# A hybrid attention and matrix-memory layer on one core: the output weights split in the first half and kept in two parts, matrix memory rows transposed at the chunk's end, the gate as tanh, another order of the projections

## The chip, the cores and the metric

The kernel runs on one core of a Trainium2 chip. The metric is the device time of one execution in microseconds (us); the kernel before took 1369.46 us in the median of three runs (1366.92 to 1369.54). A core has TensorE (PE, with its weight loads as PEld), VectorE (DVE), ScalarE (ACT), GpSimd (POOL) and SyncE (SP), which here issues all transfers. The engines run at the same time, each through its own instructions in a fixed order.

## The reference

One layer over 2048 rows of width 1024. All groups read one projection of x, each group's output is gated, and the three outputs are joined, projected and normalised:

```python
u = x @ w_in
(fq, fk, fv, ff, fz, mq, mk, mv, mi, mf, mo, mz, rq, rz) = jnp.split(u, split_points, axis=-1)
y_fox = forgetting_attention(fq, fk, fv, ff + fox_f_bias) * jax.nn.silu(fz)
...
y_ml = mlstm(mq_c, mk_c, mv, mi + i_bias, mf + f_bias, mo, norm_g) * jax.nn.silu(mz)
...
y_mem = memory_attention(rq, mem_k, mem_v) * jax.nn.silu(rz)
y = jnp.concatenate([y_fox, y_ml, y_mem], axis=-1) @ w_out
return layer_norm(DEEPNORM_ALPHA * x + y, ln_g, ln_b)
```

The first group is causal attention (6 heads of 64) with a cumulative forget bias. The second is a matrix memory (4 heads of 96) that goes through the rows in chunks and carries a state; in it h = sigmoid(o) * h, then each head is normalised (variance + 1e-5) and multiplied by norm_g. The third attends to 256 memory tokens (4 heads of 64).

## The kernel before, in words

**Precision.** Most products are made of three: an operand is rounded to a high part and the rest is kept as a low part, and high x high, low x high and high x low are summed in PSUM. So a weight tile that arrives by DMA in `raw` is split: ACT writes the high part `h`, DVE writes the low part `l` (`load_part`, line 454). The output weights of rows 384 to 767 also take the gain `norm_g` in this step (`ng_sb`).

**Stages.** The rows are two halves of 1024 (`hf`), each of two blocks of 512 (`bi`). The list `SEQ` (line 302) names the projection jobs in order for each half: `gate` (forget and input gates, attention's values), `mk`/`mv` (memory keys and values), `rq` (memory queries), `y` and `z` (gates), `h0` to `h5` (one attention head's queries and keys), `r` (matrix memory values and gates, by rows) and `c` (its queries and keys, by columns, with a convolution of four taps). A suffix `.0` or `.1` is one block alone. `u0.0` to `u3.0` in the second half lend weight buffers to the first four matrix-memory chunks.

**Attention** of a block of 512 queries of one head is an item: `att_max` computes all scores once for the maxima (PSUM `mx`, 2 banks, DVE reduces each into `mp`), `att_qk` computes them again shifted (PSUM `st`), ACT takes the exponentials twice (`ph`, `p`), DVE subtracts to the low part `pl`, POOL sums `p` into `acc` for the denominator, and `att_pv` multiplies by the values (PSUM `o`). Items follow each other in a fixed order. Keys of the first half are written to DRAM and read again for the second (`km_scr`, `kb_scr`); the block's own keys are copied by DMA (`km<-kb`, and two rows `km<-c_scr`).

**Matrix memory.** A chunk of 128 rows is one `ml_unit` (line 912), 16 in all. It reads its queries, keys, rows and gates from DRAM, makes five products in PSUM `pj` (3 banks, shared with all projections), updates the state, normalises, multiplies by the gate and writes `y_scr`.

**Output.** When the projections have freed the x buffers, `out_loads` (line 1266) loads the 16 tiles of the output weights (8 row groups by 2 column halves of 512), splitting each. `out_tile` (line 1306) handles 128 rows: it loads the transposed attention outputs from `yt_scr` in two parts (5 of the 8 row groups), loads the matrix memory's rows from `y_scr`, transposes them on PE into `st`, splits them (ACT `yh`, DVE `ylo`), multiplies by the output weights, adds alpha * x and normalises.

**What sets the order.** Every step is a generator; `Machine` (line 135) plays them against a table of costs and writes each engine's instructions in the order that this gives. Among ready steps the smallest priority (`PRIO`, line 296) goes first. On the chip that order is fixed. Every instruction is recorded by line 220 (`op.fn(...)`), so the profile is read by tile names. SP issues DMAs strictly in that order, and each waits for its data and for its buffer.

Of the kernel before, what the change touches and what calls it, by code (L numbers as in the profile page):

```python
# [12 lines left out]
F32 = mybir.dt.float32  # L13
# [3 lines left out]
ALU = mybir.AluOpType  # L17
# [259 lines left out]
class Engine:  # L277
# [5 lines left out]
    def __getattr__(self, fn):  # L283
# [11 lines left out]

PRIO = dict(load=0, wo=1.5, post=1, fin=2.5, pv=3, qk=4, mx=1.5, proj=7.5, ml=7, out=9, ln=-0.5)

# [3 lines left out]

SEQ = ("gate0 mk0.0 mk1.0 mv2.0 y0 r0 rq0 rq1.0 rq1.1 h0 y1 z0.0 h1 z0.1 z1 h2 h3 r1 h4 h5 r2 c0 c2 c5 z2 c1 c4.0 c3 c4.1",
       "rq1 rq0.1 y1 rq0.0 gate0 h0 y0.0 y0.1 r2 h1 z0 h2 r1 h3 r0 c0 u1.0 z1 u0.0 c1 h4 c4 c2 u2.0 c5.0 z2 c3 h5 c5.1 u3.0")

# [19 lines left out]
def kernel(ctx: ExitStack, tc: tile.TileContext, xt, x, wg, memt, wm, wo, cw, gb, ng, lg, lb, out):  # L324
# [96 lines left out]
    d_scr = [dram([LH, 4], F32, f"d_scr{b}") for b in range(NBLK)]  # L421
    y_scr = [dram([BLK, LW], F32, f"y_scr{b}") for b in range(NBLK)]
    yt_scr = [[dram([P, 5, BLK], F32, f"yt_scr{b}_{i}") for i in range(2)] for b in range(NBLK)]
    km_scr, kb_scr, v_scr = {}, {}, {}
# [4 lines left out]
    def loader():  # L429
        k = 0  # L430
        while True:
            yield lambda: k < len(loads)
            if loads[k] is None:
                late.append("x")
                return
            if len(loads[k]) == 2:

                tt, tag = loads[k]
                k += 1
                lent = yield [Alloc("w", [P, BLK], F32, "u") for _ in range(UNIT)]  # L440
                m.slots[tag] = [(m.wr[t.tensor.name][0], i, t) for i, t in enumerate(lent)]
                heapq.heapify(m.slots[tag])
                spawn(ml_unit(tt, 0, LH, tag), PRIO["ml"])
                continue
            src, ncol, tag, box, key, gain = loads[k]
            if k == wo_box["first"]:
                done.add("w")
            k += 1
            raw, hi, lo = yield [Alloc(RAW0 if k <= START else RAW, [P, BLK], F32, "raw"), Alloc(tag, [P, BLK], F32R, "h"),
                                 Alloc(tag, [P, BLK], F32R, "l")]  # L450
            spawn(load_part(src, ncol, raw, hi, lo, box, key, gain),
                  PRIO["load" if k <= wo_box["first"] else "wo"])

    def load_part(src, ncol, raw, hi, lo, box, key, gain):
# [435 lines left out]
    def ml_rows(g, tt, t_):  # L890
# [21 lines left out]
    def ml_unit(tt, h0, nh, tags):  # L912
# [73 lines left out]
        yield DVE.tensor_scalar(rs, mv[:, :, 1], EPS, 4.0, op0=ALU.add, op1=ALU.mult)  # L986
        yield POOL.tensor_tensor(rs2, rs, mhalf[:, 0:nh], op=ALU.pow)
# [148 lines left out]
    def rq_job(hf, w, xa, g, bi):  # L1136
# [4 lines left out]
        def post(t_):  # L1141
# [3 lines left out]
            for hh in range(2):  # L1145
# [120 lines left out]
    def out_loads():  # L1266
        wo_box.update(box={}, first=len(loads))
        for g in range(2):
            for k in KORDER:

                gain = ng_sb[:, k - 3:k - 2] if 3 <= k < 6 else None
                loads.append((wo[:, k * D + g * BLK:k * D + (g + 1) * BLK], BLK,
                              ["x"] + late if len(loads) - wo_box["first"] < EARLY else "x", wo_box["box"],
                              (KORDER.index(k), g), gain))
        loads.append(None)

# [29 lines left out]
    def out_tile(tt):  # L1306
# [3 lines left out]
        yl = yield [Alloc(["v"] + late, [P, 512], F32R, "ylo") for _ in range(2)]  # L1310
        for i, y_ in enumerate((yh, yl)):
            yield dma(out=y_[0].rearrange("p (k t) -> p k t", k=4), in_=yt_scr[b][i][:, 0:4, cs])
            yield dma(out=y_[1][:, LW:512], in_=yt_scr[b][i][:, 4, cs])
        yr = yield Alloc(late, [P, BLK], F32, "yr")
        yield dma(out=yr[:, 0:LW], in_=y_scr[b][cs, :])
        t_ = yield Alloc("st")
        yield [PE.transpose(t_[:, k * P:(k + 1) * P], yr[:, k * P:(k + 1) * P], ident) for k in range(3)]
        free(yr)
        yield ACT.copy(yh[1][:, 0:LW], t_[:, 0:LW])
        yield DVE.tensor_tensor(yl[1][:, 0:LW], t_[:, 0:LW], yh[1][:, 0:LW].bitcast(F32), op=ALU.subtract)  # L1320
        free(t_)
        zz = yield [Alloc(["raw"] + late, [P, BLK], F32, "xr") for _ in range(2)]
# [119 lines left out]
```

## Time and profile before

| | us |
|---|---|
| median of 3 runs (lowest, highest) | 1369.46 (1366.92, 1369.54) |
| the profiled execution | 1363.92 |
| its span in the trace | 1362.2 |
| PE busy | 1311.0 |
| DVE busy | 1029.7 |
| ACT busy | 650.1 |
| POOL busy | 487.8 |

The first half's projections fill about the first 480 us. The last projection job ends at 1053 us, the last attention item about 1183 us. Output tiles start at 1084.6 us, run among the attention items and have PE for themselves at the end. A matmul in the profile counts as busy until its modelled end, so neighbours overlap; lost time in PE is better read from the share of busy time in a short window together with the clock that was granted.

### The profile page before, as it was taken

How to read it: one execution, taken by the hardware profiler on the slowest of the kernel's cores; microseconds unless marked ns; L12 is line 12 of the kernel's file. 1: busy time of each engine (PE TensorE's matmuls, PEld its weight loads, DVE VectorE, ACT ScalarE, POOL GpSimd, SP SyncE). 2: the span in 40 equal slices, each digit the busy share in tenths (PEclk: the TensorE clock that was granted, in tenths of full speed). 3: DMA queues.
4: the chain of work that ended last, by engine and by line, in shares of the span. 5: the costliest groups of instructions: out<-in, count | busy, mean ns of one | idle time of the engine just before them, and what ended most of it. 6: DMA issues, size and time to landing. Idle time of an engine off the chain costs nothing.

```text
span 1362.2 us, 20386 instructions
## 1 busy us (share of the span) xinstructions
PE 1311.0 (96%) x6648; PEld 1110.4 (82%) x6648; DVE 1029.7 (76%) x2082; ACT 650.1 (48%) x1371; POOL 487.8 (36%) x430
## 2 busy tenths in 40 slices
PE   8999999999999999999999999999999798999997
PEld 7998878888888878979887889877877686788886
DVE  6647888776866688579687878988988877667755
ACT  6325545353454455323635546564565456565400
POOL 3000245242330102112526556353254178564400
PEclk9999999999999999999999999999999598999999
DMA  7614332405222452451320421315414734779642
GB/s 257 215 58 123 99 96 75 132 30 184 76 86 85 152 171 91 150 153 52 105 59 19 155 67 43 99 52 149 148 31 134 217 93 139 215 232 246 196 159 77
DMA packets 136666, 167.54 MB, mean 123 GB/s; under 512 B 13760, under 2 KB 90832, under 8 KB 136560
## 3 DMA queue, kind: packets, MB, share of 16 engines
q1 hardware_dynamic: 136560, 166.24, 39.6%
q8 instruction: 53, 0.87, 0.3%
q14 instruction: 53, 0.43, 0.1%
HBM read 107.05 MB, written 50.29 MB: 116 GB/s over the span
## 4 chain that ended last, share of the span: by engine, by line
PE 77%; DVE 12%; DMA 4%; issue 3%; ACT 2%; POOL 1%; SPq 1%; DVEq 0%; ACTq 0%; POOLq 0%
PE pj L220 57%; PE st L220 8%; PE o L220 7%; PE mx L220 5%; DVE cv L220 2%; DVE pl L220 2%; DVE l L220 2%; DMA dd<-m_scr 1%; DVE mp L220 1%; DMA raw<-in_wg_dram 1%; DMA raw<-in_xt_dram 1%; SPq L220 1%; DVE r L220 1%; POOL acc L220 1%; DVE mx L220 1%
## 5 line engine op out<-in xcount | busy, mean ns | idle before, releaser
L220 POOL TENSOR_TENSOR acc<-acc,p 128x512 f32<-128x512 f32 (+2 forms) x232 | 318.7, 1374 | 426.3 <-ACT p L220 204.9
L220 PE MATMUL pj<-h,h 128*128 128x512 f32 (+3 forms) x1144 | 424.1, 371 | 7.3 <-ACT h L220 6.5
L220 PE MATMUL pj<-h,l 128*128 128x512 f32 (+3 forms) x1144 | 418.8, 366 | 0.8 <-DVE l L220 0.7
L220 PE MATMUL pj<-l,h 128*128 128x512 f32 (+3 forms) x1144 | 419.1, 366 | 0.1
L220 PEld LDWEIGHTS pj<-h,h 128*128 128x128 f32 x1144 | 216.7, 189 | 33.3 <-ACT h L220 6.7
L220 PEld LDWEIGHTS pj<-l,h 128*128 128x128 f32 x1144 | 216.3, 189 | 28.2 <-DVE l L220 1.0
L220 PEld LDWEIGHTS pj<-h,l 128*128 128x128 f32 x1144 | 215.8, 189 | 27.2 <-DVE l L220 2.0
L220 DVE TENSOR_TENSOR pl<-p,ph 128x512 fp32r<-128x512 f32 (+2 forms) x184 | 175.3, 956 | 37.9 <-ACT p L220 33.8
L220 ACT ACTIVATE ph<-st 128x512 fp32r<-128x512 f32 (+2 forms) x219 | 120.3, 556 | 99.6 <-PE st L220 80.5
L220 DVE TENSOR_TENSOR l<-raw,h 128x512 fp32r<-128x512 f32 (+2 forms) x194 | 127.0, 681 | 31.4 <-ACT h L220 30.3
L220 ACT CAST h<-raw 128x512 fp32r<-128x512 f32 (+2 forms) x194 | 108.9, 586 | 70.9 <-DMA raw<-in_wg_dram 48.7
L220 ACT ACTIVATE p<-st 128x512 f32<-128x512 f32 (+2 forms) x232 | 125.9, 545 | 32.7 <-POOL acc L220 18.1
L220 PE MATMUL mx<-km,qm 66*128 66x512 f32 (+2 forms) x304 | 104.3, 380 | 11.1 <-DVE mp L220 9.5
L220 PE MATMUL o<-pl,v 128*128 128x512 f32 (+2 forms) x272 | 103.5, 384 | 7.8 <-DVE pl L220 7.1
L220 PE MATMUL st<-qb,kb 128*128 128x512 f32 (+2 forms) x272 | 109.4, 402 | 0.0
L220 DVE TENSOR_REDUCE mp<-mx 128x1 f32<-128x512 f32 x144 | 95.9, 684 | 16.7 <-PE mx L220 14.6
L220 PE MATMUL st<-qm,km 68*128 68x512 f32 (+2 forms) x272 | 103.2, 379 | 4.6 <-ACT p L220 4.6
L220 PE MATMUL pj<-h,yh 128*128 128x512 f32 (+1 forms) x264 | 106.7, 404 | 0.0
L220 PE MATMUL pj<-h,ylo 128*128 128x512 f32 (+1 forms) x264 | 103.0, 390 | 0.0
L220 PE MATMUL pj<-l,yh 128*128 128x512 f32 (+1 forms) x264 | 102.9, 390 | 0.0
L220 POOL TENSOR_TENSOR y<-y,zs 128x512 f32<-128x512 f32 x20 | 28.8, 1441 | 172.7 <-DVE zs L220 86.2
L220 PE MATMUL o<-ph,v 128*128 128x512 f32 (+2 forms) x219 | 82.4, 380 | 0.9 <-ACT ph L220 0.9
(199 smaller groups left out, 1937.9 us busy)
## 6 DMA issues: line engine op xcount, KB each, us to landing
raw<-in_wg_dram SPq DMA_DIRECT2D x76, 256.0 KB
raw<-in_wg_dram SPq DMA_DIRECT2D x48, 192.0 KB
v<-v_all SPq DMA_DIRECT2D x36, 256.0 KB
raw<-in_xt_dram SPq DMA_DIRECT2D x32, 256.0 KB
xr<-in_x_dram SPq DMA_DIRECT2D x32, 256.0 KB
out_dram<-xr SPq DMA_DIRECT2D x32, 256.0 KB
v_all<-vs SPq DMA_DIRECT2D x16, 384.0 KB
row_scr<-stg SPq DMA_DIRECT2D x32, 192.0 KB
```

The costliest lines, as they stand in the source:

```text
L220: op.fn(*op.args, **op.kw)
```

## The change

1. **Output weights.** Four steps `o0` to `o3` stand in the first half's list; each loads and splits four of the 16 tiles in buffers of the tag `w` and writes both parts to DRAM (`out_split`, `kept`). At the end `load_again` loads two finished parts for each tile, without ACT or DVE.
2. **Matrix memory rows.** The chunk itself transposes its 128 x 384 result on PE (into `pj`), splits it (ACT `yh`, DVE `yl`) and writes both parts to `yt_scr`, which now has all 8 row groups; the memory attention's two groups lie in places 3 and 7. `out_tile` loads two parts in four DMAs and has no transpose, no split and no `y_scr`.
3. **Gate as tanh.** The gate's `0.5 * tanh + 0.5` (one DVE instruction per 128 rows) is gone; the chunk multiplies by (1 + tanh), twice the sigmoid, and its 1e-5 becomes 4e-5 accordingly.
4. **Priority.** The first four chunks have priority 3 in place of 7.
5. **Order.** Both lists of `SEQ` are new.

```diff
-PRIO = dict(..., mx=1.5, proj=7.5, ml=7, out=9, ln=-0.5)
+PRIO = dict(..., mx=1.5, proj=7.5, ml=7, unit=3, out=9, ln=-0.5)
...
-       "rq1 rq0.1 y1 rq0.0 gate0 h0 y0.0 y0.1 r2 h1 z0 h2 r1 h3 r0 c0 u1.0 z1 u0.0 c1 h4 c4 c2 u2.0 c5.0 z2 c3 h5 c5.1 u3.0")
+       "rq1 rq0 y1 gate0 h0 z0 y0 r2 h1 h2 r1 h3 r0 c0 u1.0 z1 u0.0 c1 h4 c5.0 c4 c2 c3 u2.0 z2 c5.1 h5 u3.0")
...
+        if kept is not None:
+            for i, t_ in enumerate((hi, lo)):
+                yield dma(out=kept[i][:, :], in_=t_[:, 0:ncol])
+                if box is None:
+                    free(t_)
+            kept.append("stored")
+
+    def load_again(ncol, hi, lo, box, key, kept):
+        yield lambda: len(kept) == 3
+        for i, t_ in enumerate((hi, lo)):
+            yield dma(out=t_[:, 0:ncol], in_=kept[i][:, :])
+        box[key] = (hi, lo)
...
-            if g == 1:
-                yield DVE.tensor_scalar(o_, o_, 0.5, 0.5, op0=ALU.mult, op1=ALU.add)
-            else:
+            if g == 2:
...
-        yield DVE.tensor_tensor(hg, nd[:, :, 0:LD], hg, op=ALU.mult)
+        yield DVE.scalar_tensor_tensor(hg, hg, 1.0, nd[:, :, 0:LD], op0=ALU.add, op1=ALU.mult)
...
-        yield dma(out=y_scr[b][s * P:(s + 1) * P, h0 * LD:(h0 + nh) * LD], in_=gz[:, 0:nh * LD])
-        free(so, gz)
+        t_ = yield Alloc("pj")
+        yield [PE.transpose(t_[:, k * P:(k + 1) * P], gz[:, k * P:(k + 1) * P], ident) for k in range(3)]
+        free(gz)
+        parts = yield [Alloc(small, [P, ws], F32, s_) for s_ in ("yh", "yl")]
...
+        yield ACT.copy(h_, t_[:, 0:LW])
+        yield DVE.tensor_tensor(l_, t_[:, 0:LW], h_.bitcast(F32), op=ALU.subtract)
...
+    def out_split(n):
+        for g, i in WO_ORDER[4 * n:4 * n + 4]:
+            k = KORDER[i]
+            gain = ng_sb[:, k - 3:k - 2] if 3 <= k < 6 else None
+            wo_parts[g, i] = stored(f"wo{k}_{g}", BLK)
+            loads.append((wo[...], BLK, "w", None, None, gain, wo_parts[g, i]))
```

The order moves at two places that the prediction speaks of. The first is DVE just after the last projection, where the maxima of the last two attention items are reduced (`mp<-mx`). Before, the splits of the output weights (`l<-raw`) stand among them, and a chunk's state update (`cst`):

```order
L220 TENSOR_REDUCE mp_2779_11724<-mx_2782_11728 128x1
L220 SCALAR_TENSOR_TENSOR l_2764_11677<-raw_2762_11675,ng_sb_95,h_2763_11676 128x512
L220 CAST rr_2789_11750<-mx_2787_11745 8x128
L220 SCALAR_TENSOR_TENSOR cst0_182<-cst0_182,dec0_1087,pj_2777_11718 96x97 x2
L220 SCALAR_TENSOR_TENSOR cst1_183<-cst1_183,dec0_1087,pj_2777_11718 96x97 x2
L220 SCALAR_TENSOR_TENSOR l_2770_11695<-raw_2768_11693,ng_sb_95,h_2769_11694 128x512
L220 TENSOR_REDUCE mp_2779_11724<-mx_2788_11748 128x1
L220 SCALAR_TENSOR_TENSOR l_2776_11712<-raw_2774_11710,ng_sb_95,h_2775_11711 128x512
L220 TENSOR_TENSOR l_2786_11739<-raw_2784_11737,h_2785_11738 128x512
L220 TENSOR_REDUCE mp_2779_11724<-mx_2790_11755 128x1
```

Now, at the same item's reduces, DVE has no split of weights; between the reduces stand steps of two chunks (`dd`, and `u`, the lent buffers of the fourth):

```order
L220 TENSOR_REDUCE mp_2816_11873<-mx_2821_11883 128x1
L220 SCALAR_TENSOR_TENSOR sc_2780_11771<-sc_2780_11771 128x4
L220 CAST rr_2824_11897<-mx_2822_11889 8x128
L220 TENSOR_REDUCE mp_2816_11873<-mx_2823_11891 128x1
L220 TENSOR_REDUCE mp_2816_11873<-mx_2825_11901 128x1
L220 TENSOR_REDUCE mp_2816_11873<-mx_2826_11905 128x1
L220 TENSOR_TENSOR dd_2795_11816<-pj_2828_11917,dd_2795_11816 128x512
L220 TENSOR_REDUCE mp_2816_11873<-mx_2827_11911 128x1
L220 TENSOR_REDUCE mp_2816_11873<-mx_2831_11927 128x1
L220 TENSOR_TENSOR u_2664_11360<-u_2663_11359,u_2664_11360 128x384
```

So the splits moved out, into the first half, and the chunks' steps moved up. The second place is SP at the end of the projections. Before, the own keys of the last head's first block (`km0<-kb`, `km0<-c_scr`) stand ahead of, or among, the first loads of output weights (`raw<-in_wo_dram`):

```order
L220 DMA km0_102<-kb_2676_11422 64x512
L220 DMA raw_2688_11451<-in_wo_dram 128x512
L220 DMA raw_2691_11454<-in_wo_dram 128x512
L220 DMA raw_2694_11457<-in_wo_dram 128x512
L220 DMA y_scr0_170<-u_2478_10567 128x384
L220 DMA u_2681_11444<-qk_scr0_134 96x4x128
L220 DMA km0_102<-c_scr2_160 2x512
```

Now the own keys (here `km1`) stand behind the last ten loads of kept parts (`wo6_1` to `wo7_1`, `_h` high and `_l` low):

```order
L220 DMA u_2664_11360<-row_scr3_141 128x384
L220 DMA h_2752_11677<-wo6_1_h_196 128x512
L220 DMA l_2753_11678<-wo6_1_l_197 128x512
L220 DMA h_2754_11679<-wo3_1_h_206 128x512
L220 DMA l_2755_11680<-wo3_1_l_207 128x512
L220 DMA h_2756_11681<-wo4_1_h_208 128x512
L220 DMA l_2757_11682<-wo4_1_l_209 128x512
L220 DMA h_2758_11683<-wo5_1_h_210 128x512
L220 DMA l_2759_11684<-wo5_1_l_211 128x512
L220 DMA h_2760_11685<-wo7_1_h_212 128x512
L220 DMA l_2761_11686<-wo7_1_l_213 128x512
L220 DMA km1_103<-kb_2773_11734 64x512
```

What moved is the key copy: it is now queued behind ten loads of 256 KB. All in all SP has 64 DMAs more: 32 stores and 32 loads of the kept parts, 16 more stores of chunks and 16 fewer loads of output tiles; the 16 loads of the raw output weights stand in the first half.

More of the change, by code (lines that the diff above doesn't have):

```diff
@@ L294 @@
 YTAGS = ("ta", "pl", "ph")
-PRIO = dict(load=0, wo=1.5, post=1, fin=2.5, pv=3, qk=4, mx=1.5, proj=7.5, ml=7, out=9, ln=-0.5)
+PRIO = dict(load=0, wo=1.5, post=1, fin=2.5, pv=3, qk=4, mx=1.5, proj=7.5, ml=7, unit=3, out=9, ln=-0.5)
 EARLY = 3
@@ L421 @@
     d_scr = [dram([LH, 4], F32, f"d_scr{b}") for b in range(NBLK)]
-    y_scr = [dram([BLK, LW], F32, f"y_scr{b}") for b in range(NBLK)]
-    yt_scr = [[dram([P, 5, BLK], F32, f"yt_scr{b}_{i}") for i in range(2)] for b in range(NBLK)]
+    yt_scr = [[dram([P, KT, BLK], F32, f"yt_scr{b}_{i}") for i in range(2)] for b in range(NBLK)]
     km_scr, kb_scr, v_scr = {}, {}, {}
@@ L442, in loader @@
                 heapq.heapify(m.slots[tag])
-                spawn(ml_unit(tt, 0, LH, tag), PRIO["ml"])
+                spawn(ml_unit(tt, 0, LH, tag), PRIO["unit"])
                 continue
-            src, ncol, tag, box, key, gain = loads[k]
+            src, ncol, tag, box, key, gain, *kept = loads[k]
             if k == wo_box["first"]:
@@ L448, in loader, with load_part @@
             k += 1
+            if src is None:
+                hi, lo = yield [Alloc(tag, [P, BLK], F32R, s_) for s_ in "hl"]
+                spawn(load_again(ncol, hi, lo, box, key, *kept), PRIO["load" if k <= wo_box["first"] else "wo"])
+                continue
             raw, hi, lo = yield [Alloc(RAW0 if k <= START else RAW, [P, BLK], F32, "raw"), Alloc(tag, [P, BLK], F32R, "h"),
                                  Alloc(tag, [P, BLK], F32R, "l")]
-            spawn(load_part(src, ncol, raw, hi, lo, box, key, gain),
+            spawn(load_part(src, ncol, raw, hi, lo, box, key, gain, *kept),
                   PRIO["load" if k <= wo_box["first"] else "wo"])
-    def load_part(src, ncol, raw, hi, lo, box, key, gain):
+    def load_part(src, ncol, raw, hi, lo, box, key, gain, kept=None):
         yield dma(out=raw[:, 0:ncol], in_=src)
@@ L463, in load_part, with stored @@
         free(raw)
+        if box is not None:
+            box[key] = (hi, lo)
[9 more added lines that the diff above has]
+            yield dma(out=t_[:, 0:ncol], in_=kept[i][:, :])
         box[key] = (hi, lo)
+    def stored(name, ncol):
+        return [dram([P, ncol], F32, f"{name}_{i}") for i in "hl"]
     class Weights:
@@ L501 @@
     KORDER = (0, 1, 2, 6, 3, 4, 5, 7)
+    WO_ORDER = [(g, i) for g in range(2) for i in range(KT)]
     def proj_cols(w, xa, nfree=BLK):
@@ L985, in ml_unit @@
         yield [DVE.bn_aggr(mv[:, h, :], st6[:, h, :]) for h in range(nh)]
[L986 removed]
+        yield DVE.tensor_scalar(rs, mv[:, :, 1], 4.0 * EPS, 4.0, op0=ALU.add, op1=ALU.mult)
         yield POOL.tensor_tensor(rs2, rs, mhalf[:, 0:nh], op=ALU.pow)
@@ L992, in ml_unit @@
         yield DVE.tensor_tensor(gz[:, 0:nh * LD], so[:, 0:nh * LD], gz[:, 0:nh * LD], op=ALU.mult)
-        yield dma(out=y_scr[b][s * P:(s + 1) * P, h0 * LD:(h0 + nh) * LD], in_=gz[:, 0:nh * LD])
-        free(so, gz)
+        free(so)
+        t_ = yield Alloc("pj")
+        yield [PE.transpose(t_[:, k * P:(k + 1) * P], gz[:, k * P:(k + 1) * P], ident) for k in range(3)]
+        free(gz)
+        parts = yield [Alloc(small, [P, ws], F32, s_) for s_ in ("yh", "yl")]
+        h_, l_ = (a[:, 0:LW].bitcast(F32R) for a in parts)
+        yield ACT.copy(h_, t_[:, 0:LW])
+        yield DVE.tensor_tensor(l_, t_[:, 0:LW], h_.bitcast(F32), op=ALU.subtract)
+        free(t_)
+        for i, a in enumerate(parts):
+            yield dma(out=yt_scr[b][i][:, 4:7, s * P:(s + 1) * P],
+                      in_=a[:, 0:LW].rearrange("p (k t) -> p k t", k=3))
+            free(a)
         if tt < UNITS:
@@ L1039, in plan @@
                 continue
+            if kind == "o":
+                out_split(a)
+                continue
             if kind[0] == "m":
@@ L1046, in plan @@
                 mk = lambda: Columns(xt[2 * hf + bi], BLK, sum(g[0] == hf and g[3] == bi and g[1][0] != "m"
-                                                               for g in PROJ if g[1] != "u"), "x")
+                                                               for g in PROJ if g[1] not in "uo"), "x")
                 gi = {"gate": G_GATE, "rq": G_RQ, "y": G_RZ, "z": G_FZ, "h": G_FOX, "r": G_LROW, "c": G_LQK}[kind] + a
@@ L1267, in out_loads @@
         wo_box.update(box={}, first=len(loads))
[L1268 to L1274, printed above, removed]
-        loads.append(None)
+        for g, i in WO_ORDER:
+            loads.append((None, BLK, ("x", "w") if len(loads) - wo_box["first"] < EARLY else "x", wo_box["box"], (i, g),
+                          None, wo_parts[g, i]))
+        loads.append(None)
+    wo_parts = {}
+    def out_split(n):
[3 more added lines that the diff above has]
+            wo_parts[g, i] = stored(f"wo{k}_{g}", BLK)
+            loads.append((wo[:, k * D + g * BLK:k * D + (g + 1) * BLK], BLK, "w", None, None, gain, wo_parts[g, i]))
     wo_box = {}
@@ L1310, in out_tile @@
         yl = yield [Alloc(["v"] + late, [P, 512], F32R, "ylo") for _ in range(2)]
[L1311 to L1321, printed above, removed]
+        for j in range(2):
+            for i, y_ in enumerate((yh, yl)):
+                yield dma(out=y_[j].rearrange("p (k t) -> p k t", k=4), in_=yt_scr[b][i][:, 4 * j:4 * j + 4, cs])
         zz = yield [Alloc(["raw"] + late, [P, BLK], F32, "xr") for _ in range(2)]
```

4 lines of the change are left out of this document (2 added, 2 removed).

## Prediction

> **What bounds the kernel now.** I read the page first, then the busy time in short windows, then the groups and waits of the worst window.
>
> ```profile
> span 1362.2 us, 20386 instructions
> PE 1311.0 (96%) x6648; PEld 1110.4 (82%) x6648; DVE 1029.7 (76%) x2082; ACT 650.1 (48%) x1371; POOL 487.8 (36%) x430
> PE   8999999999999999999999999999999798999997
> DVE  6647888776866688579687878988988877667755
> PEclk9999999999999999999999999999999598999999
> DMA  7614332405222452451320421315414734779642
> PE 77%; DVE 12%; DMA 4%; issue 3%; ACT 2%; POOL 1%; SPq 1%; DVEq 0%; ACTq 0%; POOLq 0%
> ```
>
> PE carries the chain (77%) and is busy 96% of the span. The change takes no product away: the 48 transposes of the matrix memory's rows move, the rest stays. So a gain can only come from time in which PE waits or runs at a low clock. That sits in one place: slice 32 of the PE row falls to 7 and of the clock row to 5. Windows of 10 us show it (columns: engines' busy time with instruction counts, granted clock, DMA share, GB/s):
>
> ```profile
> 1040.00:1050.00 10.00, 10.00 (x49) 8.18 (x48) 6.72 (x11) 4.96 (x10) 3.62 (x4) 1.00 0.90 279
> 1050.00:1060.00 10.00, 6.74 (x30) 4.39 (x29) 9.94 (x18) 7.21 (x15) 2.04 (x2) 0.92 1.05 269
> 1060.00:1070.00 10.00, 7.35 (x35) 7.26 (x35) 8.05 (x18) 4.59 (x11) 1.44 (x2) 0.50 1.08 313
> 1070.00:1080.00 10.00, 8.04 (x31) 6.02 (x31) 7.59 (x20) 4.97 (x11) 0.00 (x0) 0.50 0.51 150
> 1080.00:1090.00 10.00, 9.42 (x24) 6.15 (x23) 8.25 (x20) 2.74 (x7) 0.00 (x0) 0.55 0.44 150
> 1090.00:1100.00 10.00, 10.00 (x45) 7.96 (x44) 9.29 (x23) 4.62 (x9) 6.32 (x5) 1.00 0.00 0
> ```
>
> From 1050 to 1090 us PE's busy time times its clock is 6.74 x 0.92 + 7.35 x 0.50 + 8.04 x 0.50 + 9.42 x 0.55 = 19.1 us in 40: 20.9 us are lost. DVE is busy 9.94 of 10 us where this begins. What DVE does from 1040 to 1090 us, by groups (count, busy us, mean ns), ACT's half of the splits, and from the page the score matmuls of the whole run:
>
> ```profile
> L220 DVE TENSOR_REDUCE mp<-mx 128x1 f32<-128x512 f32 x20 | 13.2, 681 | 3.1 <-PE mx L220 3.1
> L220 DVE TENSOR_TENSOR l<-raw,h 128x512 fp32r<-128x512 f32 x10 | 6.8, 685 | 0.1
> L220 DVE SCALAR_TENSOR_TENSOR l<-raw,ng_sb,h 128x512 fp32r<-128x512 f32 x6 | 4.3, 742 | 0.0
> L220 ACT CAST h<-raw 128x512 fp32r<-128x512 f32 x10 | 5.9, 618 | 4.7 <-DMA raw<-in_wo_dram 4.7
> L220 ACT ACTIVATE h<-raw,ng_sb 128x512 fp32r<-128x512 f32 x6 | 4.3, 722 | 0.9 <-DMA raw<-in_wo_dram 0.8
> L220 PE MATMUL mx<-km,qm 66*128 66x512 f32 (+2 forms) x304 | 104.3, 380 | 11.1 <-DVE mp L220 9.5
> ```
>
> Twenty reduces for the maxima of the last items share DVE with the 16 splits of the output weights. PE makes a score tile in 0.38 us, DVE reduces it in 0.68, and there are two banks for it, so each split in DVE's queue is a wait of PE. The timelines of DVE and of PE show it:
>
> ```profile
> 1058.71 2.07 DVE L220 SCALAR_TENSOR_TENSOR l<-raw,ng_sb,h 128x512 fp32r<-128x512 f32 x3
> 1060.70 0.69 DVE L220 SCALAR_TENSOR_TENSOR cv<-u,cv 128x512 f32<-128x512 f32 x1
> 1061.30 0.69 DVE L220 TENSOR_TENSOR l<-raw,h 128x512 fp32r<-128x512 f32 x1
> 1061.90 1.28 DVE L220 TENSOR_REDUCE mp<-mx 128x1 f32<-128x512 f32 x2
> 1058.19 0.67 PE L220 MATMUL mx<-km,qm 66*128 66x512 f32 x1
> 1062.65 0.80 PE L220 MATMUL mx<-km,qm 66*128 66x512 f32 x1 [3.79 <-DVE mp L220]
> ```
>
> Three splits, one convolution step and a fourth split keep the next reduce from 1058.7 to 1061.9, and PE stands still for 3.79 us.
>
> **The change part by part.** The sum is made against the profiled execution, 1363.92 us (span 1362.2); the median of the runs is 1369.46, 5.5 us higher, and I carry the sum over to it unchanged.
>
> *Splits out of the last stage.* 10 x 0.685 + 6 x 0.742 = 11.3 us leave DVE in the stretch where it sets PE's pace, and 5.9 + 4.3 = 10.2 us leave ACT. DVE itself is idle 6.2 us of the 40 (33.83 busy), so the relief is not less than 11.3 - 6.2 = 5.1. I take all of it, since half of DVE's idle is the reduces' own wait for PE (3.1 us in the row of `mp`), which runs at half clock: -11.3. What is late next is the reduces themselves: 20 x 0.681 = 13.6 us, and the chunk steps that the new order puts between them.
>
> *Reloads of the kept parts.* 32 loads of 256 KB stand for 16, so 4.2 MB more in this stage. The order puts the last ten (2.62 MB) ahead of the own keys of the last head's first block, and SP is a queue: behind them wait the key copy, the forget rows, the second block's keys, and then the loads of the first output tiles. At 313 GB/s (the fullest row above) ten take 8.4 us, at 269 they take 9.7. The first two thirds of that item's reduces need no own keys: 8 x 0.681 = 5.4 us. So PE waits 3.0 to 4.3 us for the keys: +3.5. The Trainium skill, DMA: Bandwidth & Descriptors, section Bandwidth, puts the fabric's limit at 435 GB/s; by that the ten would take 6.0 us and the wait be 0.6, the sum 3 us lower. The trace speaks for the dearer price: its fullest windows, at a DMA share over 1, moved 269 and 313 GB/s.
>
> *Splits into the first half.* The same 11.3 us of DVE and 10.2 of ACT, with 4.2 MB read and 8.4 MB written. By the order they stand with the heads' end and the columns' projections, between about 300 and 480 us:
>
> ```profile
> 300.00:400.00 100.00, 99.94 (x543) 88.06 (x542) 73.30 (x145) 47.12 (x97) 37.61 (x31) 1.00 0.31 101
> 400.00:480.00 80.00, 80.00 (x355) 66.24 (x354) 52.30 (x98) 37.99 (x65) 5.17 (x4) 1.00 0.41 134
> ```
>
> PE loses nothing there, DVE has 54 us free, ACT 95, and the DMA moves less than half of what it moves at 1065 us. The projections' matmuls hide it. If the cover fails (two `w` buffers are held by each tile until it is stored, and the next weights wait for them in the loader), it costs at most a quarter of the moved DVE time, some 3 us; +1.
>
> *Rows transposed in the chunk.* The same three transposes, one ACT copy and one DVE subtraction move from the tile to the chunk, and from the idle `st` banks to the three `pj` banks. Rows of before:
>
> ```profile
> L220 PE MATMUL st<-ident_r,yr x48: 270/272/476, 1076.4 to 1332.7; 128*128 128x128 f32 x48
> L220 DVE TENSOR_TENSOR ylo<-st,yh x16: 524/548/553, 1084.4 to 1334.4; 128x384 fp32r<-128x384 f32 x16
>   ACT yh L220: 48.9, 9
> ```
>
> The last row: ACT stood idle 48.9 us for these transposes, which cost nothing since ACT had no work waiting that PE needed. The DMAs have this cover in the last stage:
>
> ```profile
> 1183.00:1362.20 179.20, 170.58 (x931) 145.12 (x931) 115.92 (x309) 59.53 (x170) 60.72 (x60) 0.98 0.61 184
> 1210.00:1220.00 10.00, 10.00 (x60) 8.70 (x59) 8.06 (x19) 4.49 (x14) 6.33 (x6) 1.00 0.97 285
> 1250.00:1260.00 10.00, 10.00 (x55) 8.44 (x54) 7.56 (x37) 4.21 (x16) 1.01 (x1) 1.00 1.09 233
> ```
>
> Per chunk 192 KB more are stored (two parts), per tile 192 KB more loaded (2 x 512 KB in place of 2 x 320 and 192): 6.3 MB over 16, at 285 GB/s 22 us of DMA. It is free 39% of 179 us, 70 us, but full in some windows, where PE still lost nothing. Bounds 0 and +4 (a fifth of the 22); +1. A wait of PE for a `pj` bank is in this price.
>
> *Gate as tanh.* The removed instruction, by its row:
>
> ```profile
> L220 DVE TENSOR_SCALAR stg<-stg x16: 341/360/1452, 264.5 to 774.4; 128x384 f32<-128x384 f32 x16
> ```
>
> 16 x 0.36 = 5.8 us of DVE, done by 775 us, half of it in the first half where DVE is covered. Bounds -2 and 0; -0.5. The chunk's multiplication becomes a scalar_tensor_tensor of the same 128x384 size; nothing.
>
> *Priority and order.* The stage before the end of the projections:
>
> ```profile
> 800.00:1040.00 240.00, 230.35 (x1123) 188.74 (x1122) 211.04 (x356) 137.63 (x286) 119.55 (x93) 0.99 0.25 76
> ```
>
> PE loses 240 - 230.35 x 0.99 = 12 us here with DVE at 88%. A new order of the same work can halve or raise that by half: -6 to +6; with no row to prefer a side, 0. That the last block's convolution (`c5.1`) now stands ahead of the last head, and a third chunk's steps come into the reduces, about cancel.
>
> *Clock.* Half clock lasted from 1060 to about 1085 us. It halved (7.35 + 8.04) of busy time and took 0.45 of 9.42, some 12 us. A stretch about 8 us shorter of 40 takes a fifth of that away: -2.
>
> Sum: -11.3 + 3.5 + 1 + 1 - 0.5 + 0 - 2 = -8.3; 1363.9 becomes 1355.6, and the median 1361.
>
> **The rivals.**
>
> *The clock stays up (faster still).* If PE's gaps become short enough, the half clock never comes. For it: the drop came with gaps of DVE waits only. Against it: the reduces alone still take 0.68 us where PE takes 0.38, so PE keeps short gaps there. Then all 20.9 us of the stretch go, and with a better flow behind it up to 26: 1343 to 1349. The Trainium skill, TensorE: Matmul & The Clock Gate, section on HAM oscillation, names PE gaps over about 3.4 us as what halves the clock; by that rule the 3.79 us gap, which goes with the splits, is the cause, and this rival would hold. The trace does not quite agree: the window that ends at 1060 already has 0.92, before that gap is over. Chance 0.24.
>
> *DVE was not the price.* If the reduces' own pace and the chunk steps fill the place of the splits, relief and reload cancel: within 2.7 us of no change, 1367 to 1372. For it: DVE's idle of 6.2 us and three chunks in the wave. Chance 0.13.
>
> *The reload burst holds PE (slower).* The keys and then the first output tiles stand in SP's queue behind the reloads, two chunks' loads and the x rows. If the burst runs at 150 GB/s (as the rows 1070 and 1080 do), ten loads take 17.5 us, the keys come 12 us after their reduces could start in place of 3.5, and a PE at rest stays at half clock for some 10 us more (5 us lost): -8.3 - 3.5 + 12 + 5 = +5.2, 1375. With those 5 it decides from a wait of 6.8 us: 2.62 MB in 5.4 + 6.8 = 12.2 us, 215 GB/s. For it: small transfers stand behind big ones in one queue. Against it: 279, 269 and 313 GB/s while loads were queued; at 150 the queue had run dry. Chance 0.15.
>
> *The order costs (slower).* The new lists lose up to 6 us more in the second half, or the first half's cover fails by 3, with a normal relief: 1363 to 1373. Chance 0.06 beyond the above.
>
> **How the numbers follow.** The forecast (relief partly given back, 1356 to 1366) has 0.42. A measurement of this kernel can tell about 0.2%, 2.7 us, from no change. Faster by more: 0.42 + 0.24, with a little of the forecast's upper edge passing to the others, 0.66. Within: 0.13. Slower: 0.15 + 0.06 = 0.21. The range leaves out the far parts of the first and the third rival: 1342 to 1376.
>
> **What would show it.** In the changed kernel's windows between the last projection and the first output tile: DVE without `l<-raw`, PE's loss under 14 us in place of 20.9, the half clock shorter. The wait of `mx<-km` on the key copy or the forget rows should be 3 to 4 us; above 10 the burst rival holds. From 300 to 480 us PE should still lose under 2 us. In the last 170 us PE should lose no more than now and the DMA share be near 0.7. The prediction is wrong if the stretch is as long as before without splits on DVE, or if the time moves at another place than this one.

## The result and the profile after

The changed kernel takes 1356.3 us (median of six runs, 1354.0 to 1362.3) beside 1368.6 us of the kernel before on the same chip (median of six, the three known ahead of the prediction among them). The ratio is 0.9917, 95% interval 0.9890 to 0.9945. Timed again on another chip it was 0.9928 (0.9906 to 0.9951). That is 10 to 11 us faster by the ratios. The forecast was 1361 (1342 to 1376), 0.66 for faster: the number holds. The place that it was worked out from does not.

The page of the profiled execution (1357.78 us), the lines that answer to those of before:

```profile
span 1356.1 us, 20452 instructions
PE 1308.9 (97%) x6648; PEld 1107.4 (82%) x6648; DVE 1026.3 (76%) x2066; ACT 652.8 (48%) x1371; POOL 486.2 (36%) x430
PE   7999999999999999989999999999999799999997
PEclk9999999999999999999999999999999699999999
PE 74%; DVE 11%; DMA 6%; issue 3%; POOL 3%; ACT 2%; SPq 1%; DVEq 0%; ACTq 0%; POOLq 0%
```

Slice 32 still falls to 7, and its clock to 6. The 10 us windows of that place, in the columns of the prediction:

```profile
1040.00:1050.00 10.00, 9.95 (x55) 8.16 (x54) 7.59 (x7) 6.21 (x15) 9.25 (x8) 1.00 1.03 319
1050.00:1060.00 10.00, 9.48 (x50) 7.41 (x49) 7.03 (x7) 6.92 (x15) 8.81 (x6) 1.00 1.05 376
1060.00:1070.00 10.00, 6.30 (x24) 3.56 (x23) 9.68 (x19) 4.43 (x11) 3.03 (x4) 0.71 0.60 189
1070.00:1080.00 10.00, 7.78 (x14) 3.26 (x13) 9.43 (x32) 2.45 (x8) 1.02 (x1) 0.50 1.07 247
1080.00:1090.00 10.00, 9.64 (x33) 7.91 (x34) 6.18 (x11) 4.90 (x13) 2.87 (x4) 0.50 0.07 18
```

DVE is as full as before (9.68 and 9.43 of 10) although the 16 splits are gone. What it does from 1050 to 1090 us:

```profile
L220 DVE TENSOR_REDUCE mp<-mx 128x1 f32<-128x512 f32 x18 | 12.0, 685 | 3.0 <-PE mx L220 3.0
L220 DVE TENSOR_TENSOR pl<-p,ph 128x512 fp32r<-128x512 f32 (+2 forms) x9 | 11.6, 1293 | 3.2 <-ACT p L220 3.0
L220 DVE CUSTOM_DVE_ANT_0 mx<-mx,mrow 128x128 f32<-128x128 f32 (+3 forms) x4 | 1.9, 507 | 0.2 <-PE mx L220 0.2
```

The low parts of an attention item (`pl<-p,ph`, 11.6 us) stand where the splits stood. What PE waited for, before (1040 to 1090 us: idle in us, times, longest):

```profile
PE mx L220 <- DVE mp L220: 7.5, 8, 3.8
PE mx L220 <- DVE den L220: 0.8, 1, 0.8
```

And after (1055 to 1102 us, the three largest of five rows, which all name DVE):

```profile
PE mx L220 <- DVE mp L220: 4.2, 9, 1.7
PE o L220 <- DVE pl L220: 2.0, 3, 1.1
PE mx L220 <- DVE den L220: 0.7, 1, 0.7
```

The waits for the maxima are shorter, waits for low parts came in their place. The gain is further on, among the last attention items. Windows of 5 us of before, from 1130 us:

```profile
1130.00:1135.00 5.00, 4.62 (x30) 3.77 (x29) 4.37 (x9) 2.72 (x7) 1.95 (x3) 1.00 0.55 163
1135.00:1140.00 5.00, 2.69 (x7) 1.15 (x7) 4.97 (x13) 2.81 (x6) 5.00 (x4) 1.00 0.28 105
1140.00:1145.00 5.00, 2.73 (x8) 2.02 (x8) 4.03 (x9) 3.54 (x10) 4.92 (x5) 0.53 0.00 0
```

The same of after:

```profile
1130.00:1135.00 5.00, 5.00 (x24) 4.08 (x23) 4.09 (x6) 4.32 (x10) 5.00 (x4) 1.00 0.00 0
1135.00:1140.00 5.00, 5.00 (x25) 3.99 (x24) 1.72 (x3) 1.65 (x4) 5.00 (x5) 1.00 0.74 231
1140.00:1145.00 5.00, 5.00 (x22) 3.72 (x21) 4.32 (x7) 2.50 (x5) 5.00 (x5) 1.00 0.98 311
```

PE is fed throughout after the change; before, it has 7 and 8 matmuls in 5 us and goes to half clock. From 1135 to 1145 us the order of before has not one output product for PE, after has 31.

To see the whole, I split each run's PE time into work and loss. A matmul's work is, for its shape, the lower quartile of the time from its start to the next start in before's trace (0.23 us for 128x512); PE's work is 1242.5 us in every kernel here, and loss is time less work, counted from PE's first matmul to its last. Loss in us by stage, in the profiled executions, with the length of the stage in brackets; "output product" is a matmul of an output tile:

| | profiled, us | up to last projection | to first output product | to last attention product | to the end |
|---|---|---|---|---|---|
| before | 1363.9 | 62.0 | 20.5 (31.7) | 15.0 (79.5) | 8.4 |
| after | 1357.8 | 65.5 | 23.4 (45.8) | 3.3 (60.8) | 7.5 |
| after, second chip | 1354.8 | 63.5 | 24.4 (46.8) | 2.6 (60.1) | 6.2 |

The second run of the changed kernel was measured with the first experiments, and its expectation was:

> The changed kernel itself, beside the others on the same chip: 10 to 13 us less than before by every theory.

The stretch that the prediction spoke of lost 3 us more than before, not 8 less. The next column gained 12 us (15.0 to 3.3). The two profiled executions differ by only 6.1 us, since the first two columns took 6.4 us back.

### The profile page after: what moved, and what is told of

Same layout as the page of the kernel before. It is cut to its first block, busy times and chain, and to the rows that moved or that the text cites. A ratio compares the mean times of both kernels' runs of the same rounds, so it can differ in the third digit from the quotient of the medians.

```text
span 1356.1 us, 20452 instructions
## 1 busy us (share of the span) xinstructions
PE 1308.9 (97%) x6648; PEld 1107.4 (82%) x6648; DVE 1026.3 (76%) x2066; ACT 652.8 (48%) x1371; POOL 486.2 (36%) x430
## 3 DMA queue, kind: packets, MB, share of 16 engines
q1 hardware_dynamic: 166256, 189.32, 45.1%
## 4 chain that ended last, share of the span: by engine, by line
PE 74%; DVE 11%; DMA 6%; issue 3%; POOL 3%; ACT 2%; SPq 1%; DVEq 0%; ACTq 0%; POOLq 0%
PE pj L220 54%; PE st L220 7%; PE o L220 7%; PE mx L220 5%; DVE pl L220 2%; DVE mp L220 2%; DMA dd<-m_scr 1%; DVE l L220 1%; SPq L220 1%; POOL xr L220 1%; DVE cv L220 1%; DMA raw<-in_wg_dram 1%; DMA ylo<-yt_scr 1%; DVE r L220 1%; POOL acc L220 1%
## 5 line engine op out<-in xcount | busy, mean ns | idle before, releaser
L220 PE MATMUL pj<-h,h 128*128 128x512 f32 (+3 forms) x1144 | 425.7, 372 | 13.6 <-ACT h L220 6.4
L220 PEld LDWEIGHTS pj<-h,l 128*128 128x128 f32 x1144 | 216.2, 189 | 26.3 <-DVE l L220 0.9
L220 DVE TENSOR_TENSOR pl<-p,ph 128x512 fp32r<-128x512 f32 (+2 forms) x190 | 186.9, 989 | 31.5 <-ACT p L220 27.4
L220 DVE TENSOR_TENSOR l<-raw,h 128x512 fp32r<-128x512 f32 (+2 forms) x194 | 133.2, 712 | 38.1 <-ACT h L220 37.0
```

What stands on the lines that cost most here:

```text
L220: op.fn(*op.args, **op.kw)
```

## The experiments

Three theories stood at the start. A, the recorded one: the splits on DVE set PE's pace after the last projection. B: that stretch keeps its length whatever the weights do, and the gain is made among the last attention items. C: any edit makes the planner reorder everything, and that alone moves the time. Two kinds of kernels tell them apart: some keep every instruction in its old order (the planner counts the old cost, a shorter or an additional instruction is issued), the others are planned anew.

**1. Thin splits (before, order kept).**

```diff
-            yield DVE.tensor_tensor(lo[:, 0:ncol], raw[:, 0:ncol], hi[:, 0:ncol].bitcast(F32), op=ALU.subtract)
+            op = DVE.tensor_tensor(lo[:, 0:ncol], raw[:, 0:ncol], hi[:, 0:ncol].bitcast(F32), op=ALU.subtract)
...
+                op.less = (lo[:, 0:32], raw[:, 0:32], hi[:, 0:32].bitcast(F32))
+            yield op
```

> The kernel before with every instruction in its old order; only the 16 low-part subtractions of the output weights on DVE work on 32 of their 512 columns (POOL fills the rest of the low part with zeros, 16 fills). Left out: the low part of the output weights in 480 of each 512 columns. Some 10 us of DVE work leave the stretch between the last projection and the first output tiles and nothing takes their place. Theory A (the splits on DVE set PE's pace there, as predicted): 8 to 12 us less than before. Theory B (the stretch keeps its length without them; the change's gain was made later, in the attention tail from 1130 to 1190 us): 0 to 4 us less.

Measured: 0.9985 (0.9967 to 1.0003), 2 us less at best guess. A thin subtraction still takes 0.17 to 0.25 us (one 0.82), so 7.4 us of the 11.3 left DVE. Theory A falls: with nothing in their place, these 7.4 us were worth 4.5 at most. The 16 fills stood on POOL, and no wait of PE names them. The windows of this run show DVE relieved and PE no better off:

```profile
1060.00:1070.00 10.00, 5.09 (x23) 4.49 (x24) 5.79 (x15) 4.91 (x11) 5.52 (x12) 0.50 1.12 290
1070.00:1080.00 10.00, 9.32 (x41) 8.24 (x40) 5.46 (x24) 6.23 (x14) 1.35 (x4) 0.50 0.65 215
```

And the timelines of ACT, DVE and PE show why the largest stall got longer:

```profile
1062.83 0.62 ACT L220 CAST h<-raw 128x512 fp32r<-128x512 f32 x1 [1.23 <-DMA raw<-in_wo_dram]
1063.36 0.62 ACT L220 ACTIVATE u<-cv 128x512 f32<-128x512 f32 x1
1064.01 0.69 DVE L220 SCALAR_TENSOR_TENSOR cv<-u,cv 128x512 f32<-128x512 f32 x1 [2.12 <-ACT u L220]
1064.72 1.28 DVE L220 TENSOR_REDUCE mp<-mx 128x1 f32<-128x512 f32 x2
1065.46 0.79 PE L220 MATMUL mx<-km,qm 66*128 66x512 f32 x1 [4.91 <-DVE mp L220]
```

Read upwards: PE waits 4.91 us for a reduce, the reduce stands behind a convolution step, that waits for ACT's `u`, and ACT stood in its order behind a rounding that waited for a load. In this stall the order of the queues counts, and the load at its head, not the amount of work.

**2. Thin loads too (before, order kept).** Load, rounding and subtraction of the output weights all on 32 columns.

```diff
+            op.lesskw = dict(out=raw[:, 0:32], in_=src[:, 0:32])
...
+                op.less = (hi[:, 0:32], raw[:, 0:32])
```

> The kernel before, order kept: loads of the raw output weights, ACT's rounding and DVE's subtraction all on 32 of 512 columns (POOL fills the rest of both parts with zeros). Left out: the output weights in 480 of each 512 columns. The run with thin subtractions alone hardly gained: there DVE and ACT still waited in their order for raw weights (ACT 1.23 us for a load at 1062.8, then PE 4.9 us for a reduce). Theory F (the engines' queues wait for the loads, not for the subtractions): 6 to 12 us less than before. Theory B (the stretch keeps its length whatever the weights do, by the reduces, the chunk's steps and the half clock): 0 to 4 us less.

Measured: 0.9989 (0.9973 to 1.0004). Theory F (the queues wait for the loads of the weights) falls with A: with 7.9 us of DVE's work and most of each load gone, the stretch still lost 17.8 us of PE (29.0 long) in place of 20.5. Theory B's size holds for it. What keeps the stretch is not taken apart: PE still waits 4.9 us for reduces there, and the clock is at half from 1063.5 us on.

**3. DVE work put back (after, order kept).**

```diff
+                op = DVE.reduce_max(outs, t_[:, 0:ncol], axis=AX.X)
+                if it["i"] >= 38 and extra[0] < 8:
+                    extra[0] += 1
+                    op.more = lambda: nc.vector.tensor_tensor(mrow, mrow, mrow, op=ALU.max)
```

> The changed kernel with every instruction in its order, and 16 more DVE instructions of 128x512 (the mask row's maximum with itself, which changes nothing), one behind each of 16 plain reduces of the last two attention items: 16 x 0.68 = 11 us of DVE put back where the splits of the output weights stood. Theory A: 9 to 13 us slower than the changed kernel, so about the time of the kernel before. Theory B (DVE work in this stretch is not the price): 0 to 4 us slower than the changed kernel.

Measured: 1363.2 us beside 1356.3 of the changed kernel on the same chip (0.9990 and 0.9928 of before): 7 us slower by the medians, 8 by the ratios, between the two theories. All of it is in the stretch, which lost 31.3 us of PE in place of 24.4. In the changed order, where DVE has low parts, reduces and chunk steps in one row, 11 us more do cost 7. In the order before, 7.4 us less gave 2. So the price of DVE work there is no constant of the stretch. That it depends on whether DVE's queue stands still for something else is my reading and not shown: the added instructions also stand right behind the reduces that PE waits for, which the splits did only in part.

**4. Thin normalisation (before, order kept).** At 1141 to 1148 us of before POOL stood with one tile's layer norm; rows of its timelines (PE, ACT and POOL):

```profile
1137.84 0.50 PE L220 MATMUL st<-qm,km 68*128 68x512 f32 x1 [0.68 <-ACT p L220]
1138.22 3.14 POOL L220 TENSOR_TENSOR acc<-acc,p 128x512 f32<-128x512 f32 x2
1138.32 1.52 ACT L220 ACTIVATE xr<-xr,lsc 128x512 f32<-128x512 f32 x2 [0.53 <-DVE lsc L220]
1140.22 1.02 ACT L220 ACTIVATE n<-pj,exq 128x97 f32<-128x97 f32 x4
1141.32 3.33 POOL L220 TENSOR_TENSOR xr<-xr,lg 128x512 f32<-128x512 f32 x2
1142.27 0.79 PE L220 MATMUL st<-qm,km 68*128 68x512 f32 x1 [2.83 <-ACT p L220]
1144.61 2.97 POOL L220 TENSOR_TENSOR xr<-xr,lb 128x512 f32<-128x512 f32 x2
1148.86 0.60 ACT L220 ACTIVATE p<-st 128x512 f32<-128x512 f32 x1 [3.67 <-POOL acc L220]
```

```diff
+        if tt < 4:
+            op.less = (zg[:, 0:32], zg[:, 0:32], box["lg"][g][:, 0:32])
```

> The kernel before with every instruction in its old order; POOL's multiplication and addition of the last normalisation work on 32 of 512 columns for the first four output tiles. Left out: the layer norm's weight and bias in the other columns of rows 0 to 511. The 6.3 us in which POOL stood with one tile at 1141 to 1148 us, while ACT and then PE waited for acc<-acc,p, shrink to about 1. Theory A (the gain came from the splits): 0 to 2 us less than before. Theory B (the gain came from the attention tail, where POOL's normalisation held the exponentials): 5 to 10 us less.

Measured: 0.9972 (0.9954 to 0.9991), 2.5 us less by the medians, 4 by the ratio: between the two theories again. The 6.3 us block is gone (two `lg` take 0.83 us now), but the hole stays: its window shows PE at 6.08 of 10 at a clock of 0.60.

```profile
1140.00:1150.00 10.00, 6.08 (x15) 4.13 (x16) 8.96 (x25) 7.08 (x16) 9.81 (x11) 0.60 0.36 118
```

So POOL's block was a part, not the cause. The rows above show three parties in the same queues at once: the end of an attention item, a chunk (`n<-pj,exq`) and a normalisation (`xr<-xr,lsc`), with no output product for PE meanwhile. Why there was none is the next question. By the text of the kernel before, an output tile waits for a buffer for its rows (`yr`), then for an `st` bank, which attention items use too; the third tile's transposes came at 1143.3 us. That gave theory D: the change gains by taking this wait away.

**5 to 7. Rows in the chunk alone; the change without them; the transposes in another bank.** The first two add the part to before, and take it out of the changed kernel (there with the signs turned round):

```diff
-        yield dma(out=y_scr[b][s * P:(s + 1) * P, h0 * LD:(h0 + nh) * LD], in_=gz[:, 0:nh * LD])
...
+        t_ = yield Alloc("pj")
+        yield [PE.transpose(t_[:, k * P:(k + 1) * P], gz[:, k * P:(k + 1) * P], ident) for k in range(3)]
...
+            yield dma(out=yt_scr[b][i][:, 4:7, s * P:(s + 1) * P],
```

The third is one word in the output tile of before:

```diff
-        t_ = yield Alloc("st")
+        t_ = yield Alloc("pj")
```

> The kernel before with one part of the change alone: the chunk transposes its own rows, splits them and writes both parts to yt_scr; output weights, gate, priorities and both job lists as before. Three theories now. A (splits on DVE were the price): no change, within 2 us of before. D (before, the output tile had to get a buffer for its rows and an st bank for their transposes from the attention items, so PE had no output products to fill the attention tail at 1134 to 1146 us): most of the gain of the whole change, 7 to 13 us less than before, made between 1130 and 1190 us. C (any edit reshuffles the planner's order, and that alone moves the time): anywhere between 5 less and 5 more.

> The changed kernel without that part: output tiles load y_scr rows and transpose them in st, as before; the kept splits, the tanh gate, the priority and the new lists stay. Theory A: as fast as the changed kernel, 8 to 12 us less than before. Theory D: the gain is gone, within 4 us of before, and PE again loses some 10 us among the last attention items. Theory C: no rule.

> The kernel before with one word changed: the output tile's transposes go into a pj bank in place of an st bank. The order is the same up to the first output tile. Theory D, if the st bank is what starves PE: 3 to 10 us less, and the empty stretch without output products at 1134 to 1146 us is gone or shorter; if it is the buffer for the rows, that stretch stays and so does the time. Theory A: no change, within 2 us.

Measured: 1.0055 (1.0038 to 1.0072), 1.0057 (1.0036 to 1.0077) and 1.0077 (1.0059 to 1.0095): all three slower than before, by 7.5 to 10.5 us by the ratios, and not by what any theory with a figure gave. Theory D falls as it was put. Rows alone have a hole too, at another place (1130 to 1140 us, PE 4.80 of 10). The one word did close the hole (4.0 us lost there in place of 15.0), but the first output product came at 1104 us in place of 1085, and the last stage lost 18.0 in place of 8.4.

```profile
1130.00:1140.00 10.00, 4.80 (x12) 3.27 (x13) 8.21 (x14) 7.17 (x19) 9.55 (x8) 0.77 0.97 275
```

**8 and 9. The change without the kept splits; with the old lists and priority.**

```diff
-        for g, i in WO_ORDER:
-            loads.append((None, BLK, ("x", "w") if len(loads) - wo_box["first"] < EARLY else "x", wo_box["box"], (i, g),
-                          None, wo_parts[g, i]))
+        for g in range(2):
+            for k in KORDER:
...
```

```diff
-PRIO = dict(..., unit=3, out=9, ln=-0.5)
+PRIO = dict(..., unit=7, out=9, ln=-0.5)
...
-       "rq1 rq0 y1 gate0 h0 z0 y0 r2 h1 h2 r1 h3 r0 c0 u1.0 z1 u0.0 c1 h4 c5.0 c4 c2 c3 u2.0 z2 c5.1 h5 u3.0")
+       "rq1 rq0.1 y1 rq0.0 gate0 h0 y0.0 y0.1 r2 h1 z0 h2 r1 h3 r0 c0 u1.0 z1 u0.0 c1 h4 c4 c2 u2.0 c5.0 z2 c3 h5 c5.1 u3.0")
```

> The changed kernel without its first part: raw output weights are loaded and split in the last stage, as before, and nothing is kept from the first half; rows in the chunk, gate, priority and new lists stay. Theory A (splits on DVE were the price): 8 to 12 us slower than the changed kernel, as slow as before. Theory D2 (the gain lies among the last attention items, where output products fill PE, and needs the rows transposed in the chunk; the splits do nothing): within 4 us of the changed kernel, with under 6 us lost between the first output product and the last attention product. Theory C (any edit reorders everything and moves the time by several us): 0 to 15 us slower than the changed kernel, with the loss at any stage.

> The changed kernel with the two old job lists and the old priority of the first chunks; kept splits, rows in the chunk and gate stay. If the new lists and the priority carry the gain: 8 to 15 us slower than the changed kernel. Theory D2 (rows in the chunk carry it): within 4 us of the changed kernel. Theory C: 0 to 15 us slower, at any stage.

Measured: 1.0107 (1.0089 to 1.0126) and 0.9970 (0.9955 to 0.9986). Without the kept splits the kernel is 14.6 us slower than before, and 25 slower than the changed kernel (by the ratios to before, 1.0107 / 0.9923, the mean of the two ratios of the changed kernel). Theory D2 falls with that, and 25 us is more than A or C gave. It looks like theory A, but this kernel is planned anew, and its first output product comes only at 1118 us: until then PE works through attention and chunks without them. With the old lists and priority the kernel is 6 us slower than the changed one: less than if they carried the gain (8 to 15), more than D2 gave, inside C's bounds. The timelines of the kernel without the kept splits from 1065 us (POOL, DVE and PE):

```profile
1064.76 6.80 POOL L220 TENSOR_TENSOR acc<-acc,p 128x512 f32<-128x512 f32 x4 [0.83 <-ACT p L220]
1065.26 6.85 DVE L220 TENSOR_TENSOR pl<-p,ph 128x512 fp32r<-128x512 f32 x4
1067.09 0.51 PE L220 MATMUL o<-pl,v 128*128 128x512 f32 x1 [0.43 <-DVE pl L220]
1067.43 0.40 PE L220 MATMUL o<-ph,v 128*128 128x512 f32 x1
1067.67 0.40 PE L220 MATMUL st<-qm,km 68*128 68x512 f32 x1
1067.91 0.40 PE L220 MATMUL st<-qb,kb 128*128 128x512 f32 x1
1068.79 0.50 PE L220 MATMUL o<-pl,v 128*128 128x512 f32 x1 [0.48 <-DVE pl L220]
```

One step of attention is four matmuls, 4 x 0.23 = 0.92 us of work. It takes 1.70 us (1067.09 to 1068.79), because DVE's subtraction and POOL's sum both take 1.70 us a step (6.85 / 4 and 6.80 / 4) when they run side by side; where POOL is idle beside it, the same subtraction takes 0.68 us (median of 20 in this trace). This attention item, without filler, keeps PE at 54%. The Trainium skill, SBUF — State Buffer, section "SBUF: two separate sides", says that an instruction of DVE with two SBUF inputs and one of POOL that reads SBUF lock a shared port pair against each other for the whole instruction; equal steps of 1.70 us on both agree with that.

**10 and 11. Controls: nothing changed but the planner's assumed latency.**

```diff
-LAT, OWN = 300.0, 118.0
+LAT, OWN = 310.0, 118.0
```

> A control: the changed kernel with the planner's assumed latency between engines at 310 ns in place of 300, no instruction more or less, only another order. Theory C: the time moves by 3 to 15 us against the changed kernel, mostly up. Theories A and D2: within 3 us of it.

> The same control on the kernel before: assumed latency 310 ns, no instruction more or less. Theory C: the time moves by 3 to 10 us against before, either way. Theories A and D2: within 3 us of it.

Measured: the changed kernel becomes 1.0064 of before (1.0041 to 1.0086), some 19 us slower than itself by the ratios; the kernel before becomes 1.0147 of itself (1.0120 to 1.0174), 20 us slower. No instruction that does work was added or taken away. (The second control is written with the changed file's functions, unused; at 300 ns it gives the program of before, instruction for instruction.) Theory C holds, with more than the 3 to 15 and 3 to 10 us that it gave. At 310 ns the changed kernel is still the faster of the two, 1374.2 beside 1389.2; two orders of each are too few to say that it is so in general. The windows of the slower control show how the loss arises:

```profile
1060.00:1070.00 10.00, 5.46 (x21) 4.45 (x21) 5.93 (x10) 5.95 (x13) 0.43 (x1) 0.50 0.65 203
1070.00:1080.00 10.00, 8.33 (x24) 5.18 (x23) 8.62 (x16) 4.45 (x11) 2.90 (x3) 0.50 0.21 50
1080.00:1090.00 10.00, 7.98 (x16) 3.66 (x15) 9.44 (x34) 2.40 (x8) 0.00 (x0) 0.50 1.05 253
1120.00:1130.00 10.00, 6.94 (x22) 4.76 (x22) 9.00 (x28) 6.79 (x18) 4.74 (x4) 0.66 0.01 2
```

Its first output product comes at 1132 us, 48 us later than in before, and until then attention and chunks run without any.

The table of losses for all experiments (us, as above):

| | profiled, us | up to last projection | to first output product | to last attention product | to the end |
|---|---|---|---|---|---|
| thin splits | 1368.1 | 64.3 | 19.9 (31.1) | 15.7 (80.2) | 10.0 |
| thin loads | 1367.8 | 66.7 | 17.8 (29.0) | 14.7 (79.2) | 10.4 |
| thin normalisation | 1366.9 | 64.8 | 21.3 (32.5) | 13.5 (78.0) | 9.3 |
| after + DVE work | 1362.7 | 64.3 | 31.3 (53.7) | 2.9 (60.3) | 6.2 |
| rows alone | 1371.2 | 69.6 | 15.9 (26.3) | 13.1 (87.4) | 14.5 |
| after without rows | 1378.6 | 63.2 | 32.9 (64.4) | 9.2 (34.4) | 15.2 |
| transposes in `pj` | 1371.9 | 62.0 | 30.0 (51.6) | 4.0 (47.7) | 18.0 |
| after without kept splits | 1381.0 | 65.6 | 39.3 (69.1) | 3.1 (48.5) | 15.1 |
| after with old lists | 1363.8 | 59.8 | 29.7 (58.4) | 6.3 (44.5) | 9.9 |
| after, 310 ns | 1379.4 | 70.7 | 30.5 (59.7) | 3.0 (48.4) | 17.0 |
| before, 310 ns | 1380.4 | 64.6 | 45.1 (79.2) | 2.1 (33.5) | 10.4 |

Two regularities run through both tables. Between the last projection and the first output product PE loses 51 to 66% of the time in every order; an order with a longer stretch than before's lost 0.2 to 0.5 us more for each microsecond of that length. Once output products are there, the loss depends on how evenly they come: over the fourteen profiled runs, 5 us windows laid from the first output product on with at least ten of them lost 0.27 us each (97 windows), those with four to nine 0.63 (60), those with three or fewer 2.5 (18). Before and after have about the same number in the stretch (3 x 45 and 3 x 49), but before spends them over 77 us with 15 us of none (1131 to 1146), after over 61 us with no gap over 4.2 us.

That output products are the filler is read from these traces; no experiment moved them alone. Which part of the change makes the good order stays open too: undoing the rows costs 18 us against the changed kernel and undoing the kept splits 25, but the control, which undoes nothing, costs 19. Undoing the lists and the priority costs 6. None of these can be called the price of a part.

## Why the prediction was right or wrong

- *Splits out of the last stage, -11.3.* This step failed, at "I take all of it, since half of DVE's idle is the reduces' own wait". With order kept, 7.4 us of relief were worth 2 us (4.5 at most), so the splits were not worth what they took. Whether 5.1, called the least, would hold for all 11.3 no run tells. A full engine in a window was taken for the pace of PE; the run with thin splits shows the queue standing still for ACT with DVE at 5.79 of 10.
- *Reloads of the kept parts, +3.5.* They cost nothing that the waits show. The burst ran at 319 and 376 GB/s (windows 1040 and 1050), not at the 269 to 313 it was priced by, and most of it ran while the last projections still fed PE. The waits of PE in this stretch name DVE alone, no load and no key copy; 3 to 4 us were forecast.
- *Splits into the first half, +1.* Over the first 480 us of PE's work before lost 20.7 us, the changed kernel 23.7, and the changed kernel without the kept splits 24.5, so nothing shows that the 3 us more are the splits'. From 300 to 480 us PE was busy 179.57 of 180 us, as forecast.
- *Rows and their transfers, +1.* The last stage lost 7.5 us beside 8.4, at a DMA share of 0.70 from 1163 us on, so the 6.3 MB more are hidden, as forecast. The transposes were called free because ACT had idled for them. The price held a wait of PE for a `pj` bank, but nothing for what the row buffer and the bank do to the order of the output products; the one-word run shows that this is not one number either, since it closed the hole and lost more elsewhere.
- *Gate, -0.5.* Not tried alone.
- *Priority and order, 0 with bounds of 6.* Undoing the new lists and the priority cost 6 us, at the edge of the bounds. But every part of the change gives the planner another order, and for that there was no term: a change of nothing but the order moved the time by 19 and 20 us. The order is where the result comes from, as far as the runs show; which part of the change makes it stays open. The loss ahead of the last projection moved by 1.5 to 3.5 us. The 12 us came among the last attention items, where the prediction had no term.
- *Clock, -2.* The half clock of before lasted from 1058.4 to 1089.1 us, not from 1060 to about 1085, as the recorded windows show (0.92 and 0.55). It did shorten, mostly at another place: half clock between 1050 and 1200 us lasted 30.7 + 6.8 + 3.4 us before and 27.3 after; 10.2 of the 13.6 us that went are in the hole and at the end of the attention, not in the stretch.
- *A row read wrongly.* "PE makes a score tile in 0.38 us" is the mean busy time of a group of mixed shapes, whose neighbours overlap; at full clock the starts of 128x512 score tiles lie 0.23 us apart. It changes no term.
- *Rivals.* "DVE was not the price" came nearest to the true mechanism of its stretch, and its time, 1367 to 1372, was wrong, since it took the rest of the program as fixed. "The clock stays up" did not come, nor did the burst. The prediction named its own tests: PE's loss in the stretch under 14 us (it was 23.4), and no move of the time "at another place than this one". By both its reasoning was wrong, and the right number was luck: -8.3 was added up around a relief of 11.3 that did not come, and 12 us came from a place without a term.

## What to carry to other kernels

With a planner that sets the order, first run the unchanged kernel with one planning number altered that touches no instruction: if that moves the time by more than the effect you forecast, price the edit with the order kept, and treat the new order as a term of its own with that spread. A full engine next to a starved one is not yet the pace: ask whether its queue stands still for something else. And where one kind of work alone feeds the matrix engine at half, look for what else it can be given; here the orders that spread it evenly lost least, which no run tried by itself.

## What the runs showed of the hardware

- The clock halved without a long gap. In the changed kernel it dropped at 1064.1 us for 27.3 us; the longest wait of PE in the 16 us ahead of it was 1.06 us:

```profile
1063.86 0.57 PE L220 MATMUL o<-pl,v 128*128 128x512 f32 x1 [1.06 <-DVE pl L220]
1067.40 0.79 PE L220 MATMUL mx<-km,qm 66*128 66x512 f32 x1 [1.68 <-DVE mp L220]
```

 The rule cited with the first rival (the Trainium skill, TensorE: Matmul & The Clock Gate, section on HAM oscillation: gaps over about 3.4 us) does not cover this. In before, too, the clock dropped ahead of the gap that the prediction laid to that rule: at 1058.4 us, when the 3.79 us wait began at 1058.9 and the longest wait in the 16 us ahead was 0.77 us. What makes it drop is not shown; PE had a few short waits ahead of it at both places. Once down, PE stayed at half while it was busy 22.09 us of 27:

```profile
1064.00:1091.00 27.00, 22.09 (x59) 14.05 (x60) 21.89 (x56) 10.10 (x26) 3.89 (x5) 0.50 0.50 116
```

- DVE's 128x512 subtraction of two SBUF tiles takes 1.70 us a step beside POOL's addition of the same size (without the kept splits, from 1065 us), and 0.68 us where POOL is idle.
